# One encoder layer in float32 halves: TensorE's order, the place of the quarters' sums, the loads of the way out and the buffers of the mixer's squares

## The chip, the core and the metric

The kernel runs on one core of a Trainium2 chip. The metric is the device time of one execution in microseconds (us), as the median of several runs. Before the change it is 913.55 us (three runs, 912.46 to 914.88).

## What is computed

The reference is one layer of a bidirectional encoder over 528 tokens (512 and 16 meta tokens) of width 1024, batch 1, in float32:

```
h = concat(meta, x)
h = h + 0.5 * swiglu(rms_norm(h, norm_ffn1), w_ffn1_in, w_ffn1_out)
u = rms_norm(h, norm_mix) @ w_in
xc = conv(u[:, :512]);  y_lru = (scan_fwd(xc) + scan_bwd(xc)) * gelu(u[:, 512:1024])
y_four = fft2(u[:, 1024:]).real @ fourier_w + fourier_b
h = h + concat(rms_norm(y_lru), rms_norm(y_four)) @ w_out
h = h + 0.5 * swiglu(rms_norm(h, norm_ffn2), w_ffn2_in, w_ffn2_out)
out = rms_norm(h, norm_final)[16:]
```

The two feed-forwards have width 2816, which is 22 blocks ("f") of 128 columns for the gate and 22 for the up side.

## The kernel before, in words

**Halves.** Every operand of a matmul is split into a high and a low float32r part, and a product is three matmuls (`mm3`, L351): high by high, high by low, low by high. The high part of a weight is a ScalarE copy, the low part a VectorE subtraction (`split_w`, L89, whose instructions have lines L90 and L91; for plain blocks L333 and L334).

**Fast products in the feed-forward.** Most f blocks use a scheme with seven products instead of eight: the gate and up weights are four quarters, and seven products P1 to P7 of sums of quarters by sums of token halves give the result (`pair`, L584). The first three f blocks of the first feed-forward and the first two of the second are plain ("classic"). In the second feed-forward the way out of four chunks of four f blocks uses the same scheme (`way_out`, L649), and the first chunk (two f blocks) and the last one use plain products.

**A block's weights.** `pair_loads` (L100) brings a pair of f blocks' columns in with five DMAs into three raw buffers a, b, c: up's first half into c, gate into b, up into a (SP's queue), and then two accumulating DMAs from POOL's queue, gate's first half onto c (L108) and gate's second half onto b's first (L109). `pair_blocks` (L112) splits a, and the second half of b into the tiles jh and jl. It gives the weights of P1, P2 and P4. `pair_sums` (L122) adds c's first half to b's second half (L126), splits b, and forms c's second half from a and b (L129). It gives P6 and P5. `pair_differences` (L132) splits c for P7 and P3.

**Jobs.** All weights are a list of jobs, in the order in which they are used (`ffn_jobs`, L263). `block()` (L339) hands out the next one, keeps loads six jobs ahead (`FETCH`) and splits three jobs ahead (`LOOK`). There are seven raw buffers of 1024 columns (`wraw`) and five pairs of split tiles (`wsp`). Every plain job takes one raw buffer and one pair, however few columns it has. The way out of the first chunk of the second feed-forward is eight jobs (one for each of eight output blocks d) of 2 x 128 columns. The last chunk (`tail`, L1170) takes four jobs of 1024 columns, two outputs in each.

**The order of work.** The kernel is written with a tile framework. It takes the instructions in the order in which the program traces them, plans for each engine an order from expected times, lets an instruction whose inputs are expected move ahead of one whose inputs are not, and sets the semaphores. `tc.keep_in_program_order` ties an instruction behind the one traced before it on the same engine. In the second feed-forward the first matmul of each product group is tied so (`onto`, L569, which passes `pinned` to `mm3`):

```
            mm = nc.tensor.matmul(o, wh, xh[i], start=first, stop=False, skip_group_check=go_on)
            if pinned:
                tc.keep_in_program_order(mm)
...
                    mm3([ps], w[0][:, k], w[1][:, k], [xh], [xl], first and k == 0, k == nk - 1, True, not lead and k == 0)
```

In the first feed-forward (`lead` is set) and everywhere else TensorE's matmuls are not tied. The written order of the second feed-forward's steps is `schedule2` (L227): P1, P2, P6, P7, P5, P4, P3 of a block with way-out products of the chunk before between them. P4 adds onto the bank C that P7 wrote and that VectorE reads at L611, after P5 and ScalarE's copy L610. P3 adds onto the bank A that L610 reads.

**The mixer's norms.** `add_square` (L450) squares a block on ScalarE (L458) into a temporary and adds it to a running sum on VectorE (L459). For the LRU half (L1099) the temporary is the tag "sq" with one buffer. For the Fourier half (L1076) it is in turn that one and the tag "t" of the mixer's pool (two buffers, also used for convolutions, folds and the spread root). After the sums, TensorE adds over partitions (L467), ScalarE and VectorE take the reciprocal root, and TensorE spreads it (L485).

Of the kernel before, what the change touches and what calls it, by code (L numbers as in the profile page):

```python
# [9 lines left out]
F32 = mybir.dt.float32  # L10
# [4 lines left out]
P = 128  # L15
# [50 lines left out]
def encoder_layer(ctx: ExitStack, tc: tile.TileContext, xT, vecs, w1i, w1o, wm, wg, wo, w2i, w2o, w2q,  # L66
# [45 lines left out]
    def pair_blocks(pair):  # L112

        a, b, _ = pair["raw"]
        hi, lo = w_tiles()
        split_w(hi, lo, a)
        jh = state["pool"].tile([P, 512], F32R, tag="jh", name="jh")
        jl = state["pool"].tile([P, 512], F32R, tag="jl", name="jl")
        split_w(jh, jl, b[:, 512:])
        return [(quarter(hi, 0), quarter(lo, 0)), (quarter(hi, 1), quarter(lo, 1)), (quarter(jh, 0), quarter(jl, 0))]  # L120

    def pair_sums(pair):  # L122

        a, b, c = pair["raw"]

        tc.keep_in_program_order(nc.vector.tensor_tensor(b[:, 512:], b[:, 512:], c[:, :512], op=ALU.add))  # L126
        hi, lo = w_tiles()
        split_w(hi, lo, b)
        nc.vector.tensor_tensor(c[:, 512:], a[:, 512:], b[:, 512:], op=ALU.add)  # L129
        return [(quarter(hi, 0), quarter(lo, 0)), (quarter(hi, 1), quarter(lo, 1))]  # L130
# [132 lines left out]
    def ffn_jobs(wi, wo_, wq, steps):  # L263
        pairs = {}
        for step in steps:
            kind, f, d = step[:3]
            if kind == "out" and (len(step) == 3 or step[3] == 0):
                jobs.append((wo_[d][:, f[0]:f[1], :], P, f[1] - f[0], P, 8))
            elif kind == "tail":
                for dp in range(ND // 2):  # L270
                    src = wo_[2 * dp:2 * dp + 2, :, f[0]:f[1], :].rearrange("d p f m -> p d (f m)")
                    jobs.append((src, P, 2, (f[1] - f[0]) * P, 8))
            elif kind == "classic":
                for b in range(2):
                    jobs.append((wi[f, b], P, 8, P, 2 if len(jobs) < 3 else 8))
            elif kind == "in" and d in ("P1", "P6", "P7"):
                pair = pairs.setdefault(f, {"src": (wi[f, 1], wi[f, 0])})
                jobs.append(({"P1": pair_blocks, "P6": pair_sums, "P7": pair_differences}[d], pair))
            elif kind == "so" and d in ("P1", "P6"):
                quad = pairs.setdefault(("so", f), {"src": wq[f[0], f[2]] if d == "P1" else None})  # L280
                jobs.append((quad_blocks if d == "P1" else quad_sums, quad))
# [68 lines left out]

    def mm3(outs, wh, wl, xh, xl, first, last, go_on=False, pinned=False):  # L351

        for i, o in enumerate(outs):
            mm = nc.tensor.matmul(o, wh, xh[i], start=first, stop=False, skip_group_check=go_on)  # L354
            if pinned:
                tc.keep_in_program_order(mm)
        for i, o in enumerate(outs):
# [92 lines left out]
    def add_square(ss, src, n, first, tag="sq"):  # L450
        if first:
            nc.scalar.activation(ss[:, :n], src, AF.Square)
        else:
            if isinstance(tag, str):
                sq = tmp.tile([P, T], F32, tag=tag, bufs=1, name="sq")
            else:
                sq = tag.tile([P, T + 4], F32, tag="t", bufs=2, name="sq")
            nc.scalar.activation(sq[:, :n], src, AF.Square)  # L458
# [11 lines left out]
    def rstd_of(q, name, pool=None):  # L470
        r = tmp.tile([P, T], F32, tag="rstd", bufs=1, name=name) if pool is None else pool.tile([P, T + 4], F32, tag="t", bufs=2, name=name)
        m, k = q.shape
# [27 lines left out]
    def ffn(X, R, t0, n, steps, on_done, tail, lead, sums, hook):  # L500
        half = n // 2
        with tc.tile_pool(name="ffn", bufs=10 if lead else 3) as fp, tc.tile_pool(name="ffnt", bufs=2) as ft:
# [66 lines left out]
            def onto(ps, w, x, first):  # L569

                nk = w[0].shape[1]
                for k in range(nk):
                    xh, xl = x(k)
                    mm3([ps], w[0][:, k], w[1][:, k], [xh], [xl], first and k == 0, k == nk - 1, True, not lead and k == 0)

# [156 lines left out]
            first = []  # L732
            out = {}
            for step in steps:
# [24 lines left out]
                else:  # L759
                    if len(step) == 3 or step[3] == 0:  # L760
                        out[d] = banks(n, "po"), block()
                    ps, (wh, wl) = out[d]
                    for k, j in enumerate(range(*f)):
                        if len(step) == 3 or step[3] == k:
                            ah, al = acts[j]
                            ah, al = flat(ah), flat(al)
                            mm3(ps, wh[:, k], wl[:, k], halves(ah, n), halves(al, n), k == 0, j == f[1] - 1)
                            last = j == f[1] - 1
                    if not last:
                        continue  # L770
                    for hl, p in zip(halves(h[d][:, t0:], n), ps):
# [83 lines left out]
    with tc.tile_pool(name="mx", bufs=1) as mx, tc.tile_pool(name="mt", bufs=2) as mt:  # L855
# [219 lines left out]
        for c in range(NL):  # L1075
            add_square(ssf, yf[c][:, META:T], SEQ, c == 0, mt if c % 2 else "sq")  # L1076

# [19 lines left out]
        for c, gt in enumerate(gates):  # L1097
            nc.vector.tensor_tensor(hs[c], hs[c], gt, op=ALU.mult)
            add_square(ssl, hs[c], SEQ, c == 0)  # L1099

# [69 lines left out]
    def tail(acts, temps):  # L1170
        blocks = []
        for _ in range(ND // 2):
            parts = [x.rearrange("p d (f m) -> p d f m", m=P) for x in block()]
            blocks += [[x[:, e] for x in parts] for e in range(2)]
        nt = len(acts)
# [180 lines left out]
```

## Time and profile before

| what | value |
|---|---|
| median of three runs | 913.55 us |
| profiled execution | 917.13 us, its span 915.3 us |
| TensorE clock granted, mean | 0.991 |
| ScalarE busy | 478.9 us, 52% of the span |
| GpSimd busy | 96.7 us, 11% |
| DMA | 125.20 MB in 53744 packets, 137 GB/s |

A profile is of one execution. TensorE is PE (its weight loads PEld), VectorE DVE, ScalarE ACT, GpSimd POOL, SyncE SP; L126 is line 126 of the kernel. The clock is the share of TensorE's full speed that was granted in a stretch. Matmuls are pipelined and their ends are modelled, so counts of matmuls in a stretch tell more than the busy time does.

### The profile page before, as it was taken

To read this page: it belongs to the slowest core of one execution; us is meant where nothing else is said; L and a number is where in the kernel's file an instruction comes from. 1 tells how busy PE (TensorE), PEld (TensorE's weight loads), DVE (VectorE), ACT (ScalarE), POOL (GpSimd) and SP (SyncE) were. 2 spreads that over 40 slices of the span, in tenths; PEclk is the share of its full clock that TensorE was granted. 3 is DMA by queue.
4 is the path that set the end of the run, shared out by engine and by line. 5 is a ranking of instruction groups with operands and counts; after the bars stand their busy time and mean duration, and the time that the engine had idled before them with its cause. 6 is when DMAs were issued, how large, how long until landed. Compare 5 with 4: busy or idle time off the path is not lost.

```text
span 915.3 us, 17225 instructions
## 1 busy us (share of the span) xinstructions
PE 873.1 (95%) x6854; PEld 848.2 (93%) x6854; DVE 705.1 (77%) x1227; ACT 478.9 (52%) x766; POOL 96.7 (11%) x114
## 2 busy tenths in 40 slices
PE   8999999999999999999898999899898998898996
PEld 8999999999999999999777899798898998898996
DVE  7988765867767767678985688688878969968854
ACT  7665433534444435588545354465545545555544
POOL 0111010010010000000000000111212121131100
PEclk9999999999999999999998999999999999999998
DMA  8747653564664433431423311675586785685512
GB/s 299 180 119 189 167 150 81 159 165 105 173 161 123 132 100 114 139 106 59 138 93 81 77 33 30 184 193 154 136 217 138 161 198 139 168 203 134 159 22 92
DMA packets 53744, 125.20 MB, mean 137 GB/s; under 512 B 5920, under 2 KB 12832, under 8 KB 53664
## 3 DMA queue, kind: packets, MB, share of 16 engines
q1 hardware_dynamic: 37280, 96.84, 33.6%
q0 software_dynamic: 15840, 26.75, 18.1%
q8 instruction: 53, 0.87, 0.4%
q10 hardware_dynamic: 544, 0.52, 0.2%
q14 instruction: 27, 0.22, 0.1%
HBM read 115.70 MB, written 2.10 MB: 129 GB/s over the span
## 4 chain that ended last, share of the span: by engine, by line
PE 71%; DVE 18%; ACT 4%; issue 4%; DMA 2%; SPq 1%; DVEq 0%; ACTq 0%
PE pp L354 14%; PE pp L360 13%; PE pp L358 13%; PE po L354 5%; PE po L360 5%; PE po L358 5%; DVE wlo L91 4%; PE pw L358 2%; PE pm L354 2%; PE pm L360 1%; PE pm L358 1%; PE pw L360 1%; PE pw L354 1%; ACT whi L90 1%; DVE al L411 1%
## 5 line engine op out<-in xcount | busy, mean ns | idle before, releaser
L90 ACT ACTIVATE whi<-raw 128x1024 fp32r<-128x1024 f32 (+1 forms) x149 | 150.6, 1032 | 73.5 <-DVE raw L126 35.6
L91 DVE TENSOR_TENSOR wlo<-raw,whi 128x1024 fp32r<-128x1024 f32 (+1 forms) x149 | 175.4, 1192 | 17.2 <-ACT whi L90 17.1
L360 PE MATMUL pp<-th,wlo 128*128 128x256 f32 (+1 forms) x468 | 132.7, 284 | 3.2 <-DVE wlo L91 3.2
L354 PE MATMUL pp<-th,whi 128*128 128x256 f32 (+1 forms) x468 | 133.4, 285 | 1.2 <-ACT whi L90 0.6
L358 PE MATMUL pp<-xl,whi 128*128 128x256 f32 (+1 forms) x468 | 132.5, 283 | 0.0
L360 PE MATMUL pp<-xh,wlo 128*128 128x256 f32 (+1 forms) x468 | 132.5, 283 | 0.0
L354 PE MATMUL pp<-xh,whi 128*128 128x256 f32 (+1 forms) x468 | 132.3, 283 | 0.0
L358 PE MATMUL pp<-tl,whi 128*128 128x256 f32 (+1 forms) x468 | 132.1, 282 | 0.0
L333 ACT ACTIVATE whi<-raw 128x512 fp32r<-128x512 f32 (+3 forms) x95 | 69.4, 740 | 60.0 <-PE po L358 23.4
L360 PEld LDWEIGHTS pp<-th,wlo 128*128 128x128 f32 x468 | 88.0, 188 | 3.9 <-DVE wlo L91 3.9
L354 PEld LDWEIGHTS pp<-th,whi 128*128 128x128 f32 x468 | 88.2, 189 | 2.7 <-ACT whi L90 1.0
L334 DVE TENSOR_TENSOR wlo<-raw,whi 128x512 fp32r<-128x512 f32 (+3 forms) x95 | 78.2, 827 | 13.6 <-ACT whi L333 12.4
L354 PEld LDWEIGHTS pp<-xh,whi 128*128 128x128 f32 x468 | 88.3, 189 | 0.0
L360 PEld LDWEIGHTS pp<-xh,wlo 128*128 128x128 f32 x468 | 88.2, 189 | 0.0
L358 PEld LDWEIGHTS pp<-tl,whi 128*128 128x128 f32 x468 | 88.2, 188 | 0.0
L358 PEld LDWEIGHTS pp<-xl,whi 128*128 128x128 f32 x468 | 88.1, 188 | 0.0
L354 PE MATMUL po<-ah,whi 128*128 128x264 f32 (+1 forms) x368 | 78.8, 292 | 3.1 <-ACT whi L333 3.0
L360 PE MATMUL po<-ah,wlo 128*128 128x264 f32 (+1 forms) x368 | 78.2, 290 | 0.9 <-DVE wlo L334 0.9
L358 PE MATMUL po<-al,whi 128*128 128x264 f32 (+1 forms) x368 | 78.6, 291 | 0.0
L360 PE MATMUL pp<-ah,wlo 128*128 128x256 f32 x224 | 63.7, 285 | 3.9 <-DVE wlo L91 3.9
L354 PE MATMUL pp<-ah,whi 128*128 128x256 f32 x224 | 64.1, 286 | 1.2 <-ACT whi L90 0.7
L358 PE MATMUL pp<-al,whi 128*128 128x256 f32 x224 | 63.2, 282 | 0.0
(254 smaller groups left out, 2180.2 us busy)
## 6 DMA issues: line engine op xcount, KB each, us to landing
raw<-in_w2i SPq DMA_DIRECT2D x44, 512.0 KB, 4.4
raw<-in_w1i SPq DMA_DIRECT2D x41, 512.0 KB, 4.3
raw<-in_w2i POOLq DMA_DIRECT2D x40, 256.0 KB, 3.9
raw<-in_w1i POOLq DMA_DIRECT2D x38, 256.0 KB, 4.9
raw<-in_w1o SPq DMA_DIRECT2D x32, 256.0 KB, 3.1
raw<-in_w2q SPq DMA_DIRECT2D x16, 512.0 KB, 5.3
raw<-in_wm SPq DMA_DIRECT2D x12, 512.0 KB, 3.6
raw<-in_w2i SPq DMA_DIRECT2D x20, 256.0 KB, 3.4
```

The costliest lines, as they stand in the source:

```text
L90: nc.scalar.activation(hi, raw, AF.Copy)
L91: nc.vector.tensor_tensor(lo, raw, hi.bitcast(F32), op=ALU.subtract)
L333: nc.scalar.activation(hi[:p, s], raw[:p, s], AF.Copy)
L334: nc.vector.tensor_tensor(lo[:p, s], raw[:p, s], hi[:p, s].bitcast(F32), op=ALU.subtract)
L354: mm = nc.tensor.matmul(o, wh, xh[i], start=first, stop=False, skip_group_check=go_on)
L358: nc.tensor.matmul(o, wh, xl[i], start=False, stop=False, skip_group_check=go_on)
L360: nc.tensor.matmul(o, wl, xh[i], start=False, stop=last, skip_group_check=go_on)
L411: nc.vector.tensor_tensor(lo, src, hi.bitcast(F32), op=ALU.subtract)
```

## The change

It does four things. It takes the `pinned` parameter out, so that no matmul is tied in the second feed-forward. It moves the two additions of `pair_sums` into `pair_blocks`, behind the split of jh and jl; the first one stays tied to VectorE's traced order. It makes the way out of the second feed-forward's first chunk two jobs of 1024 columns, four outputs in each, which a new `blocks_of` hands out one by one (the tail uses it too). And it gives the mixer's squares two buffers "sq" of their own in the mixer's pool, and the spread roots two "root" buffers; both no longer use "t", and the LRU half's squares no longer the single "sq". The rest is the removal of a case that no step uses.

```diff
     def pair_blocks(pair):
 
-        a, b, _ = pair["raw"]
+        a, b, c = pair["raw"]
...
         split_w(jh, jl, b[:, 512:])
+
+        tc.keep_in_program_order(nc.vector.tensor_tensor(b[:, 512:], b[:, 512:], c[:, :512], op=ALU.add))
+        nc.vector.tensor_tensor(c[:, 512:], a[:, 512:], b[:, 512:], op=ALU.add)
...
     def pair_sums(pair):
 
-        a, b, c = pair["raw"]
-
-        tc.keep_in_program_order(nc.vector.tensor_tensor(b[:, 512:], b[:, 512:], c[:, :512], op=ALU.add))
         hi, lo = w_tiles()
-        split_w(hi, lo, b)
-        nc.vector.tensor_tensor(c[:, 512:], a[:, 512:], b[:, 512:], op=ALU.add)
+        split_w(hi, lo, pair["raw"][1])
...
-            if kind == "out" and (len(step) == 3 or step[3] == 0):
+            if kind == "out" and not wq:
                 jobs.append((wo_[d][:, f[0]:f[1], :], P, f[1] - f[0], P, 8))
-            elif kind == "tail":
-                for dp in range(ND // 2):
-                    src = wo_[2 * dp:2 * dp + 2, :, f[0]:f[1], :].rearrange("d p f m -> p d (f m)")
-                    jobs.append((src, P, 2, (f[1] - f[0]) * P, 8))
+            elif kind == "tail" or kind == "out" and d == 0:
+                m = (f[1] - f[0]) * P
+                n = 1024 // m
+                for dp in range(0, ND, n):
+                    jobs.append((wo_[dp:dp + n, :, f[0]:f[1], :].rearrange("d p f m -> p d (f m)"), P, n, m, 8))
...
-    def mm3(outs, wh, wl, xh, xl, first, last, go_on=False, pinned=False):
+    several = []
+
+    def blocks_of():
+
+        if not several:
+            parts = [x.rearrange("p d (f m) -> p d f m", m=P) for x in block()]
+            several.extend([x[:, e] for x in parts] for e in range(parts[0].shape[1]))
+        return several.pop(0)
+
+    def mm3(outs, wh, wl, xh, xl, first, last, go_on=False):
 
         for i, o in enumerate(outs):
-            mm = nc.tensor.matmul(o, wh, xh[i], start=first, stop=False, skip_group_check=go_on)
-            if pinned:
-                tc.keep_in_program_order(mm)
+            nc.tensor.matmul(o, wh, xh[i], start=first, stop=False, skip_group_check=go_on)
...
-                sq = tag.tile([P, T + 4], F32, tag="t", bufs=2, name="sq")
+                sq = tag.tile([P, T], F32, tag="sq", bufs=2, name="sq")
...
-        r = tmp.tile([P, T], F32, tag="rstd", bufs=1, name=name) if pool is None else pool.tile([P, T + 4], F32, tag="t", bufs=2, name=name)
+        r = tmp.tile([P, T], F32, tag="rstd", bufs=1, name=name) if pool is None else pool.tile([P, T], F32, tag="root", bufs=2, name=name)
...
-                    mm3([ps], w[0][:, k], w[1][:, k], [xh], [xl], first and k == 0, k == nk - 1, True, not lead and k == 0)
+                    mm3([ps], w[0][:, k], w[1][:, k], [xh], [xl], first and k == 0, k == nk - 1, True)
...
-                    if len(step) == 3 or step[3] == 0:
-                        out[d] = banks(n, "po"), block()
-                    ps, (wh, wl) = out[d]
+                    ps, (wh, wl) = banks(n, "po"), block() if lead else blocks_of()
...
-            add_square(ssf, yf[c][:, META:T], SEQ, c == 0, mt if c % 2 else "sq")
+            add_square(ssf, yf[c][:, META:T], SEQ, c == 0, mt)
...
-            add_square(ssl, hs[c], SEQ, c == 0)
+            add_square(ssl, hs[c], SEQ, c == 0, mt)
...
     def tail(acts, temps):
-        blocks = []
-        for _ in range(ND // 2):
-            parts = [x.rearrange("p d (f m) -> p d f m", m=P) for x in block()]
-            blocks += [[x[:, e] for x in parts] for e in range(2)]
+        blocks = [blocks_of() for _ in range(ND)]
```

## Rows read from the trace of the kernel before

**Rows 1.** The page, part 1: busy us and share of the span of each engine.

```profile
PE 873.1 (95%) x6854; PEld 848.2 (93%) x6854; DVE 705.1 (77%) x1227; ACT 478.9 (52%) x766; POOL 96.7 (11%) x114
```

**Rows 2.** Stretches: length, busy us (instructions) of each engine, clock, DMA share, GB/s.

```profile
61.00:345.00 284.00, 283.84 (x2321) 283.10 (x2320) 206.99 (x340) 125.77 (x190) 26.91 (x31) 1.00 0.55 143
479.00:490.70 11.70, 11.57 (x50) 8.86 (x48) 10.51 (x16) 9.19 (x14) 0.00 (x0) 1.00 0.23 69
490.70:495.50 4.80, 2.03 (x10) 1.66 (x8) 1.82 (x2) 2.86 (x3) 0.87 (x1) 0.75 0.40 82
495.50:500.40 4.90, 4.90 (x13) 3.90 (x14) 0.18 (x1) 0.26 (x1) 0.86 (x1) 0.55 0.39 117
540.00:564.70 24.70, 23.74 (x200) 23.77 (x201) 22.69 (x49) 13.33 (x23) 0.00 (x0) 1.00 0.06 17
564.70:581.80 17.10, 13.24 (x50) 9.84 (x49) 10.95 (x20) 6.10 (x11) 0.00 (x0) 0.90 0.20 57
581.80:616.00 34.20, 33.07 (x276) 32.62 (x275) 27.24 (x43) 17.28 (x28) 6.96 (x8) 1.00 0.84 223
616.00:662.00 46.00, 41.84 (x343) 40.81 (x343) 40.43 (x70) 26.05 (x41) 7.90 (x9) 1.00 0.59 147
662.00:682.00 20.00, 20.00 (x169) 19.93 (x168) 16.28 (x30) 11.22 (x18) 4.39 (x5) 1.00 0.92 222
```

**Rows 3.** Timeline of ScalarE, 486 to 493 us: start, us, what, idle before and releaser.

```profile
487.81 0.63 ACT L458 ACTIVATE sq<-t 128x512 f32<-128x512 f32 x1 [0.22 <-DVE ss L459]
490.88 1.06 ACT L333 ACTIVATE whi<-raw 128x1024 fp32r<-128x1024 f32 x1 [2.44 <-PE pw L358]
491.84 0.61 ACT L458 ACTIVATE sq<-t 128x512 f32<-128x512 f32 x1
```

**Rows 4.** Timeline of TensorE, 486 to 505 us, a wait.

```profile
493.85 1.87 PE L467 MATMUL sums<-consts,ss 128*128 128x1 f32 x8 [2.77 <-DVE ss L459]
```

**Rows 5.** Timeline of SyncE's queue, 500 to 640 us: the loads of the way out.

```profile
539.07 36.55 SPq L306 DMA_DIRECT2D raw<-in_w2o  x8
```

**Rows 6.** Timeline of ScalarE, 568 to 581 us.

```profile
574.39 0.42 ACT L333 ACTIVATE whi<-raw 128x256 fp32r<-128x256 f32 x1 [4.49 <-DMA raw<-in_w2o]
```

**Rows 7.** DMA issues: count, KB each, median us to landing.

```profile
raw<-in_w2i SPq DMA_DIRECT2D x44, 512.0 KB, 4.4
...
raw<-in_w2o SPq DMA_DIRECT2D x8, 128.0 KB, 2.0
```

**Rows 8.** Waits of TensorE, 581 to 862 us: us in total, times, longest.

```profile
PE pp L354 <- DVE q L611: 9.9, 10, 1.6
PE pp L360 <- DVE wlo L91: 7.1, 7, 1.3
```

**Rows 9.** Timeline of TensorE, 632 to 662 us, three of its waits.

```profile
636.50 0.39 PE L360 MATMUL pp<-ah,wlo 128*128 128x256 f32 x1 [0.96 <-DVE wlo L91]
...
641.34 0.39 PE L354 MATMUL pp<-th,jh 128*128 128x256 f32 x1 [1.27 <-DVE q L611]
...
653.52 0.39 PE L360 MATMUL pp<-th,wlo 128*128 128x256 f32 x1 [0.95 <-DVE wlo L91]
```

**Rows 10.** Timeline of VectorE, 24 to 34 and 620 to 664 us.

```profile
26.53 0.68 DVE L91 TENSOR_TENSOR jl<-raw,jh 128x512 fp32r<-128x512 f32 x1
...
633.62 0.69 DVE L91 TENSOR_TENSOR jl<-raw,jh 128x512 fp32r<-128x512 f32 x1
...
635.23 2.08 DVE L91 TENSOR_TENSOR wlo<-raw,whi 128x1024 fp32r<-128x1024 f32 x2
...
650.17 0.69 DVE L126 TENSOR_TENSOR raw<-raw 128x512 f32<-128x512 f32 x1
```

**Rows 11.** Timeline of GpSimd, 18 to 34 and 540 to 640 us: accumulating transfers issued.

```profile
21.91 1.02 POOL L108 DMA_DIRECT2D raw<-in_w1i  x1 [21.46 <-DMA raw<-in_w1i]
...
621.00 0.86 POOL L108 DMA_DIRECT2D raw<-in_w2i  x1 [12.29 <-DMA raw<-in_w2i]
```

**Rows 12.** Line L108, the first accumulating transfer of each block: time to landing.

```profile
DMA to landing us min/median/max: 3.5/3.9/7.7
```

More of the change, by code (lines that the diff above doesn't have):

```diff
@@ L732, in ffn @@
             first = []
-            out = {}
             for step in steps:
@@ L759, in ffn @@
                 else:
-                    if len(step) == 3 or step[3] == 0:
-                        out[d] = banks(n, "po"), block()
-                    ps, (wh, wl) = out[d]
+                    ps, (wh, wl) = banks(n, "po"), block() if lead else blocks_of()
                     for k, j in enumerate(range(*f)):
[L764 to L770, printed above, removed]
+                        ah, al = [flat(x) for x in acts[j]]
+                        mm3(ps, wh[:, k], wl[:, k], halves(ah, n), halves(al, n), k == 0, j == f[1] - 1)
                     for hl, p in zip(halves(h[d][:, t0:], n), ps):
```

## The prediction

> **What bounds the kernel now.** I read the page first. TensorE is busy 95% of the span, the engine next to it, VectorE, 77% [rows 1], so the question is where TensorE runs below its pace. The stretches answer that [rows 2]. From 61 to 345 us, the first feed-forward block, it has no idle time: 2321 matmuls in 284 us, 0.122 us each. Nothing is pinned there. In the second block a light stretch (662 to 682) runs 169 matmuls in 20 us, 0.118 us each, and that is the pace I measure the rest by. Three places fall short.
>
> First, the mixer's norm. In 4.8 us from 490.7 only 10 instructions run, and in the 4.9 us after it 13 run at a granted clock of 0.55 [rows 2]. TensorE waits 2.77 us for the last add into ss [rows 4]. On ScalarE the second square through the one "sq" buffer waits for VectorE's add, and the third stands behind a weight split that waits 2.44 us for TensorE [rows 3].
>
> Second, the way out of the first two f blocks: 564.7 to 581.8 holds its 48 products of 512 columns (8 outputs x 2 f blocks x 3) in 17.1 us, with a clock of 0.90 [rows 2]. Its eight loads are spread over 36.55 us [rows 5], and ScalarE waits 4.49 us for one of them [rows 6], though one lands in 2.0 us [rows 7]. The buffers are the cause: two blocks that are fetched ahead hold six of the seven raw buffers, so each 256-column load waits until the load before it has been split.
>
> Third, the rest of the second block. From 581 to 862 us the two largest waits of TensorE are for the add of L611 and for low halves (L91) [rows 8]. One period shows them in place [rows 9]: at 636.5 a low half, at 641.3 the add, at 653.5 a low half. From 616 to 662 us there are 343 matmuls in 46 us; at 0.118 they need 40.6, so 5.4 are lost [rows 2]. The pattern comes four times (616, 682, 747 and 813 us). From 581.8 to 616 us, 276 matmuls need 32.7 of 34.2: 1.5 lost. Together 4 x 5.4 + 1.5 = 23.1 us. VectorE is nearly full in that heavy stretch: 40.43 us of 46, and 16.28 of 20 in the light one [rows 2].
>
> **The change part by part.**
>
> *Own buffers for squares.* With two "sq" buffers the second square needs no add, and the third needs the add that held the second one before, at 487.81 [rows 3]. That is 3 us ahead of the split at 490.88, if ScalarE's planned order lets it go first. Then the last add ends near 490, and the sums need not wait: 2.8 us [rows 4]. The half-clock stretch behind the wait goes too: 12 products of 512 columns take 4.9 us there, and at the pace ahead of 490.7 (50 in 11.70 us, 0.234 each [rows 2]) 2.8: 2.1 us. Sum 4.9. Bounds: 0, where the split keeps its place before the third square, and 4.9. I take 4.9, since nothing else in those rows holds the squares. The final reciprocal root and its spread hide behind the next products as they do now. Moving the other squares off the "t" buffers I cost at nothing: TensorE has projections to run there.
>
> *Way out by 1024 columns.* Eight loads, eight ScalarE and eight VectorE splits of 256 columns become two of 1024. A 512 KB load lands in 4.4 us [rows 7]; the first is issued at 539, the second when the first is split, near 557, so it lands near 562 and feeds the fifth of eight outputs, near 570. The wait and the half clock go: 48 x 0.234 = 11.2 us against 17.1, 5.9 us. SP issues six DMAs fewer, and the raw buffers come free earlier for the next blocks. Against this, VectorE has 2.8 us more to do before 565 (next part), where it is busy 22.69 of 24.7 us [rows 2] and has 2.0 left: 0.8 late. Sum 5.1; bounds 2 (a second load that comes as late as the worst ones now, for half the outputs) and 5.9.
>
> *Sums with the first three blocks.* Nothing is added: two VectorE adds of 0.69 us move from the preparation of P6 to that of P1. In the row's period they go from 650.17 and the next to it to just behind the low half at 633.62 [rows 10]. P6's split then no longer waits for them, and the raw buffer of "up" is free some 17 us earlier, so SP's and POOL's queues move up too. The price: the low half at 635.23, for which TensorE waits at 636.5 [rows 9], would start 1.4 us later, four times: 5.6 us. The gain is the wait at 653.5, 0.95 us, four times: 3.8. Lasting bounds are thus -5.6 and +3.8; I take 0, because a free order of products (next part) can cover the later split. For the first two blocks of the second feed-forward the adds (2.8 us) land between 541 and 545 us, which is the 0.8 above.
> The accumulating transfer that the add reads was issued at 621.00 [rows 11] and at the longest landing of 7.7 us [rows 12] is there by 628.7, five us before the add would run; by these rows the move makes no wait. Only at the very start can it: the transfer issued at 21.91 [rows 11] may land as late as 29.6, and the low half before the add begins at 26.53 [rows 10], so VectorE may stand up to 2.4 us. TensorE has 144 classic products of the first blocks to run then (17.6 us at 0.122), which hide it; without them it would cost 2.4, and I take 0. The Trainium skill's page "Perfetto Trace Analysis", section "Per-engine timelines", says that VectorE takes its instructions strictly first in, first out, which speaks against the move: an add whose transfer is late holds every split behind it. By that rule alone the sum would lose wherever a transfer is late; no row shows one so late.
>
> *Order no longer pinned.* The pin ties the first product of each group (P1 to P7 of a block and of a way-out square) behind all products before it. Without it the framework, when it plans the order, may put any product ahead whose inputs it expects. While P4 waits for L611, P3 needs only ScalarE's copy, and the next way-out products need only their weights; while a low half is late, P5 or the next block's P1 can run. So there is work for each of the waits. But VectorE must supply it: without the 5.4 us the heavy stretch would be 40.6 us long with 40.43 of VectorE work in it, 99.6%. Over heavy and light stretch together it would be 56.7 of 60.6, 94%, so part of the work has to move over, as far as five split buffers and seven raw ones allow. Bounds: 0 (the waits are VectorE's and stay) and 23.1 (all go). I take 60%, 13.9 us: nearer to the upper end, because in the unpinned first block no TensorE time is lost, and short of it for VectorE's sake. Should a stall go, the low halves are late next.
>
> Sum: 4.9 + 5.1 + 13.9 = 23.9 us. The profiled execution took 917.13 us, 3.6 more than the median of the runs, 913.55. 917.1 - 23.9 = 893.2; on the median's scale 889.6.
>
> **The rivals.**
>
> *All waits go.* For it: the unpinned first block. Against it: VectorE at 94%. It gains 23.1 + 10.0 = 33.1: 880.5 on the median's scale, within 877 to 884.
>
> *VectorE is the bound.* The order changes but the products still wait for low halves, which come as before. For it: 40.43 of 46 us, and two waits of three are for VectorE's splits or adds. It leaves 0 to 7 us of the third part's 23.1: 913.6 - 10.0 - 4 = 899.6 in the middle, 897 to 906 with the low bounds of the first two parts.
>
> *A product planned ahead of its turn stops the queue (slower).* The order is fixed at build time by expected times. If the planner puts a product early and its weights come later on the chip, everything behind it stands, and no pin keeps it behind. Place: the five chunks of the second block. Price: as at 490.7, a wait of 2.8 us and 2.1 lost at half clock, 4.9 us. One in each chunk, and nothing gained in the third part, gives 24.5 - 10 = 14.5: 928; two in each give 953. It decides once three such stalls stand without a gain in the third part: then they eat the 10 us of the first two. For it: TensorE stands at 490.7 and in the way out with unpinned products, so its planned order is not always right. Against it: the first block. The Trainium skill's page "TensorE: Matmul & The Clock Gate", section "Step-by-step: what each phase is for", says that the queue pulls only weight loads ahead and that matmuls stay in program order; the trace agrees, since no product ran during the 2.77 us of that wait [rows 4].
>
> *It changes nothing.* The planner finds the same order, and ScalarE's order keeps the split ahead of the square; new small waits eat what the loads bring: 911 to 916.
>
> **How the numbers follow.** Forecast (7 to 19 us of the third part, 884 to 897) 0.48; all waits go 0.15; VectorE the bound 0.22; nothing 0.04; slower 0.11. A measurement of this kernel can tell about 0.3%, 2.7 us, from no change. Faster by more: 0.48 + 0.15 + 0.22 = 0.85; within it 0.04; slower 0.11. The range 876 to 906 takes in the first three cases, 0.85, with the bounds of the single terms.
>
> **What the profile after would show.** Squares right: no wait of TensorE for ss before the second half's sums, and the clock at 1.00 there. Loads right: two loads of w2o of 512 KB ahead of the tail's, and 48 products of 512 columns in 11 to 12 us. Sums right: L126's successor directly behind the low half of each third quarter, and ScalarE no longer waiting for it. Order right: P4 no longer directly behind P5 and two way-out products, waits for L611 under a third of the 9.9 us now, and VectorE busy over 90% of the four periods. The forecast is wrong if TensorE's waits in the second block stay above 15 us, or if new waits on DMA or on ScalarE's high halves appear there.

## The result, and the profile after

The changed kernel takes 889.71 us, the median of four runs (889.41 to 891.26), against 914.21 of the kernel before beside it: ratio 0.9738, 95% interval 0.9718 to 0.9757. Its profiled execution is the one of 889.71 us, span 887.9. The profiled execution of before (917.13) was 2.9 us above its median, this one is on its own, so 27.4 us less in the two spans stand for 24.5 in the medians.

Lines have moved: L121 and L122 are the sums (L126, L129 before), L363/L365/L367 the three matmuls of `mm3`, L376 a product (`times`), L417/L418 the split of an activation (L410, L411), L465/L466 square and add, L474 the sums over partitions, L618 the add of P4 (L611). L90/L91 and L333/L334 are still the weight splits.

The page, part 1, which answers to [rows 1]:

```profile
PE 869.8 (98%) x6854; PEld 847.1 (95%) x6854; DVE 700.1 (79%) x1221; ACT 476.4 (54%) x760; POOL 96.7 (11%) x114
```

Stretches of the changed kernel, against [rows 2] (columns: stretch, length; busy us and instructions of PE, PEld, DVE, ACT, POOL; granted clock, DMA share, GB/s):

```profile
61.00:345.00 284.00, 283.79 (x2321) 283.01 (x2321) 207.78 (x341) 125.96 (x191) 25.90 (x30) 1.00 0.55 140
490.70:495.50 4.80, 4.80 (x31) 4.17 (x30) 1.41 (x2) 2.60 (x3) 0.87 (x1) 1.00 0.45 102
534.00:558.80 24.80, 23.59 (x199) 23.62 (x200) 24.31 (x49) 13.25 (x20) 1.73 (x2) 1.00 0.38 96
561.70:574.50 12.80, 12.78 (x48) 10.05 (x49) 9.45 (x14) 2.32 (x4) 1.75 (x2) 0.87 0.61 151
574.60:605.00 30.40, 30.32 (x255) 30.11 (x254) 21.27 (x34) 15.35 (x24) 3.47 (x4) 1.00 0.52 130
605.00:645.00 40.00, 39.96 (x333) 39.40 (x332) 36.32 (x65) 24.14 (x38) 6.13 (x7) 1.00 0.62 161
666.00:727.00 61.00, 60.92 (x506) 60.11 (x505) 53.69 (x96) 35.28 (x57) 14.10 (x16) 1.00 0.78 185
```

The first block is the same to 0.05 us of TensorE. From 574.6 to the tail at 850 the view lists no wait of TensorE: 40 us hold 333 matmuls, 0.120 each, where before 46 us held 343. VectorE, the feared bound, is at 36.32 of 40 there and at 53.69 of 61 (88%) over a full period.

TensorE's waits after 470 us, all that the view lists (engine and line, releaser: us in total, times, longest); the two of [rows 8] are gone, and a new one leads; the last is at the very end, in the final norm:

```profile
PE po L363 <- ACT ah L417: 2.6, 1, 2.6
PE sums L474 <- DVE ss L466: 1.5, 1, 1.5
PE pss L492 <- DVE root L1225: 0.6, 1, 0.6
```

**The norm.** Timeline of ScalarE, 484 to 495 us (start, us, what, idle before and releaser), against [rows 3]:

```profile
486.07 1.24 ACT L465 ACTIVATE sq<-t 128x512 f32<-128x512 f32 x2
487.22 1.05 ACT L333 ACTIVATE whi<-raw 128x1024 fp32r<-128x1024 f32 x1
488.17 0.61 ACT L465 ACTIVATE sq<-t 128x512 f32<-128x512 f32 x1
490.98 1.06 ACT L333 ACTIVATE whi<-raw 128x1024 fp32r<-128x1024 f32 x1 [2.20 <-PE pw L365]
```

The third square now stands ahead of the split that waits for TensorE. VectorE's last add into ss starts at 489.70 and takes 0.68, and the sums run at 491.01 without a wait.

**The way out.** Its two loads are issued one behind the other (SyncE's queue, start, us between first and last):

```profile
533.32 5.79 SPq L306 DMA_DIRECT2D raw<-in_w2o  x2
```

They are early, against 36.55 us [rows 5], and no weight is late. But the first product waits for an activation and the clock falls behind it. Timeline of TensorE:

```profile
561.72 1.41 PE L363 MATMUL po<-ah,whi 128*128 128x512 f32 x4 [2.63 <-ACT ah L417]
...
563.85 0.63 PE L363 MATMUL po<-ah,whi 128*128 128x512 f32 x1
...
565.96 0.40 PE L363 MATMUL po<-ah,whi 128*128 128x512 f32 x1
```

Steps of 0.42 us from 563.4 to 566.0, 0.23 behind it: the half clock (1.2 of 2.4 GHz). What ScalarE and VectorE did before it, and, last, TensorE's first product of P1 of the fast blocks, from which the text below counts:

```profile
553.92 1.04 ACT L90 ACTIVATE whi<-raw 128x1024 fp32r<-128x1024 f32 x1
...
556.76 1.05 ACT L90 ACTIVATE whi<-raw 128x1024 fp32r<-128x1024 f32 x1
...
559.12 1.08 ACT L714 ACTIVATE q<-pg 128x512 f32<-128x512 f32 x2
560.09 1.06 ACT L90 ACTIVATE whi<-raw 128x1024 fp32r<-128x1024 f32 x1
561.04 1.15 ACT L417 ACTIVATE ah<-q 128x512 fp32r<-128x512 f32 x2
...
558.45 1.22 DVE L91 TENSOR_TENSOR wlo<-raw,whi 128x1024 fp32r<-128x1024 f32 x1
559.75 1.29 DVE L376 TENSOR_TENSOR q<-pu,q 128x512 f32<-128x512 f32 x2
560.96 1.21 DVE L91 TENSOR_TENSOR wlo<-raw,whi 128x1024 fp32r<-128x1024 f32 x1
562.09 1.29 DVE L418 TENSOR_TENSOR al<-q,ah 128x512 fp32r<-128x512 f32 x2
...
553.23 0.28 PE L363 MATMUL pp<-xh,whi 128*128 128x256 f32 x1
```

On ScalarE three weight splits stand ahead of ah: P6's of the first two fast blocks (553.92 and 556.76) and the next in the list of jobs, P7's of the first (560.09). On VectorE P6's low halves are at 558.45 and 560.96. Their products run only behind the 48 of the way out. What TensorE waits for is ah, so it is ScalarE's order that counts: ah starts 7.81 us after the first product of P1 (561.04 against 553.23). The Trainium skill's page "Perfetto Trace Analysis", section "Per-engine timelines", has ScalarE and VectorE take their instructions strictly first in, first out; the trace agrees, since q, whose last product into pg starts at 552.75, comes on ScalarE only at 559.12, behind two of the splits.

**Where the time came from.** Marks of the profiled executions in us, with the runs' medians and ratios (A: first product after the norm, `pw` from yl; B: first product of the way out; C: the product behind its 48th; D: first product of the tail, `pt`):

```
kernel                 median  ratio [95%]             A       B       C       D       B-A    C-B    D-C    span
before                 914.21                          504.08  564.71  581.84  877.40  60.63  17.13  295.56 915.3
after                  889.71  0.9738 [0.9718,0.9757]  498.38  561.72  574.60  850.25  63.34  12.88  275.65 887.9
b1_unpin               898.46  0.9808 [0.9789,0.9827]  503.86  564.40  580.74  859.10  60.54  16.34  278.36 896.9
b2_sums_early          908.20  0.9914 [0.9901,0.9927]  504.13  566.32  577.71  869.70  62.19  11.39  291.99 907.5
b3_loads_1024          908.47  0.9924 [0.9902,0.9947]  501.31  562.31  573.61  867.65  61.00  11.30  294.04 905.4
b4_squares             911.79  0.9947 [0.9929,0.9966]  498.52  560.63  577.71  871.93  62.11  17.08  294.22 909.7
a1_pins_back           907.65  0.9910 [0.9892,0.9928]  498.37  563.30  576.11  868.09  64.93  12.81  291.98 905.8
a2_sums_late           888.82  0.9706 [0.9687,0.9725]  498.29  559.32  570.58  848.95  61.03  11.26  278.37 887.2
a3_loads_256           887.40  0.9690 [0.9671,0.9709]  499.24  561.26  572.64  848.22  62.02  11.38  275.58 886.0
a4_squares_back        894.16  0.9767 [0.9748,0.9786]  503.32  566.66  579.47  855.00  63.34  12.81  275.53 892.6
r_after                889.76  0.9714 [0.9695,0.9733]  498.44  561.79  574.38  849.96  63.35  12.59  275.58 887.6
c1_two_late            887.42  0.9687 [0.9668,0.9705]  498.41  560.89  572.18  847.75  62.48  11.29  275.57 885.6
c3_p6_tied             887.35  0.9685 [0.9672,0.9698]  498.13  560.59  571.83  847.75  62.46  11.24  275.92 885.5
c2_two_late_norm       885.50  0.9667 [0.9654,0.9679]  498.23  558.85  570.11  845.74  60.62  11.26  275.63 884.1
```

Against before the change gains 5.70 us up to A, loses 2.71 between A and B, gains 4.25 from B to C and 19.91 from C to D, and 0.26 behind D: 27.4.

### The profile page after: what moved, and what is told of

It reads as the page before. It is cut to its first block, busy times and chain, and to the rows that moved or that the text cites. A ratio compares the mean times of both kernels' runs of the same rounds, so it can differ in the third digit from the quotient of the medians.

```text
span 887.9 us, 17188 instructions
## 1 busy us (share of the span) xinstructions
PE 869.8 (98%) x6854; PEld 847.1 (95%) x6854; DVE 700.1 (79%) x1221; ACT 476.4 (54%) x760; POOL 96.7 (11%) x114
## 4 chain that ended last, share of the span: by engine, by line
PE 83%; DVE 10%; ACT 4%; issue 2%; DMA 1%; SPq 1%; DVEq 0%; ACTq 0%
PE pp L363 17%; PE pp L365 16%; PE pp L367 16%; PE po L363 5%; PE po L365 5%; PE po L367 5%; PE pm L365 2%; PE pm L363 2%; PE pm L367 2%; PE pw L365 2%; PE pw L367 1%; PE pw L363 1%; DVE wlo L91 1%; ACT whi L90 1%; PE pt L363 1%
## 5 line engine op out<-in xcount | busy, mean ns | idle before, releaser
L90 ACT ACTIVATE whi<-raw 128x1024 fp32r<-128x1024 f32 (+1 forms) x149 | 150.9, 1032 | 85.1 <-PE po L365 32.7
L91 DVE TENSOR_TENSOR wlo<-raw,whi 128x1024 fp32r<-128x1024 f32 (+1 forms) x149 | 176.3, 1193 | 10.8 <-ACT whi L90 9.8
L363 PE MATMUL pp<-xh,whi 128*128 128x256 f32 (+1 forms) x468 | 132.5, 285 | 1.3 <-ACT whi L90 0.5
L363 PE MATMUL pp<-th,whi 128*128 128x256 f32 (+1 forms) x468 | 133.3, 285 | 0.3
L365 PE MATMUL pp<-xl,whi 128*128 128x256 f32 (+1 forms) x468 | 132.5, 283 | 0.0
L367 PE MATMUL pp<-xh,wlo 128*128 128x256 f32 (+1 forms) x468 | 132.3, 283 | 0.0
L365 PE MATMUL pp<-tl,whi 128*128 128x256 f32 (+1 forms) x468 | 132.0, 282 | 0.0
L367 PE MATMUL pp<-th,wlo 128*128 128x256 f32 (+1 forms) x468 | 131.9, 283 | 0.0
L333 ACT ACTIVATE whi<-raw 128x512 fp32r<-128x512 f32 (+3 forms) x89 | 68.2, 777 | 51.9 <-PE po L365 23.8
L363 PEld LDWEIGHTS pp<-xh,whi 128*128 128x128 f32 x468 | 88.0, 189 | 3.2 <-ACT whi L90 1.5
L363 PEld LDWEIGHTS pp<-th,whi 128*128 128x128 f32 x468 | 88.2, 188 | 1.6 <-ACT q L599 1.2
L365 PEld LDWEIGHTS pp<-tl,whi 128*128 128x128 f32 x468 | 88.2, 188 | 0.0
L367 PEld LDWEIGHTS pp<-xh,wlo 128*128 128x128 f32 x468 | 88.2, 188 | 0.0
L365 PEld LDWEIGHTS pp<-xl,whi 128*128 128x128 f32 x468 | 88.1, 188 | 0.0
L367 PEld LDWEIGHTS pp<-th,wlo 128*128 128x128 f32 x468 | 87.9, 188 | 0.0
L334 DVE TENSOR_TENSOR wlo<-raw,whi 128x512 fp32r<-128x512 f32 (+3 forms) x89 | 77.2, 873 | 11.7 <-ACT whi L333 10.7
L363 PE MATMUL po<-ah,whi 128*128 128x264 f32 (+1 forms) x368 | 78.1, 291 | 2.7 <-ACT ah L417 2.6
L365 PE MATMUL po<-al,whi 128*128 128x264 f32 (+1 forms) x368 | 78.6, 291 | 0.0
L367 PE MATMUL po<-ah,wlo 128*128 128x264 f32 (+1 forms) x368 | 78.3, 291 | 0.0
L363 PE MATMUL pp<-ah,whi 128*128 128x256 f32 x224 | 63.7, 288 | 0.0
L365 PE MATMUL pp<-al,whi 128*128 128x256 f32 x224 | 63.0, 282 | 0.0
L367 PE MATMUL pp<-ah,wlo 128*128 128x256 f32 x224 | 62.3, 283 | 0.0
```

The source lines that it names most:

```text
L90: nc.scalar.activation(hi, raw, AF.Copy)
L91: nc.vector.tensor_tensor(lo, raw, hi.bitcast(F32), op=ALU.subtract)
L333: nc.scalar.activation(hi[:p, s], raw[:p, s], AF.Copy)
L334: nc.vector.tensor_tensor(lo[:p, s], raw[:p, s], hi[:p, s].bitcast(F32), op=ALU.subtract)
L365: nc.tensor.matmul(o, wh, xl[i], start=False, stop=False, skip_group_check=go_on)
L367: nc.tensor.matmul(o, wl, xh[i], start=False, stop=last, skip_group_check=go_on)
```

## The experiments

The runs came in three groups, each beside runs of the kernel before (medians 915.37, 916.67 and 915.66). "a" and "c" kernels are the changed kernel edited, "b" kernels the one before. A gain of a "b" kernel is given by its ratio; the medians alone differ by 18.2 us (b1), 7.5 (b2), 8.2 (b3) and 3.9 (b4).

**The free order: a1_pins_back and b1_unpin.** The same lines, put back into the one and taken out of the other:

```diff
-            nc.tensor.matmul(o, wh, xh[i], start=first, stop=False, skip_group_check=go_on)
+            mm = nc.tensor.matmul(o, wh, xh[i], start=first, stop=False, skip_group_check=go_on)
+            if pinned:
+                tc.keep_in_program_order(mm)
```

> The changed kernel with the first matmul of each product group tied again in the second feed-forward, all else as changed. Theory 1 (the free order of TensorE brings the 20 us gained between the first P6 and the tail): the four periods go back from 61.1 to about 65 us, the kernel to 905 to 911. Theory 2 (the early sums bring them, since P6's split no longer waits for L126 and a raw buffer is free sooner): the periods stay under 62.5 us, the kernel under 896. Both needed: in between, and the run with late sums shows as much.

> The kernel before with the ties taken away and nothing else. Theory 1 (the free order alone removes the waits of the four periods): the waits after 582 us go, 17 to 21 us less than before on the same chip (894 to 898), with the waits at 493 and 574 us still there. Rival (it takes the early sums too): 5 to 12 us less.

Measured: with the pins back, 907.65 us, 17.9 more than the changed kernel; with nothing but the pins gone, 0.9808, that is 17.6 of 916.67 less. C to D takes 291.98 us against 275.65, and 278.36 against 295.56: 16.3 and 17.2. (b1_unpin's 898.46 is 0.5 above the 894 to 898 expected, the difference within its 17 to 21; its waits at 493 and near 574 us stay, 2.8 and 2.6.) TensorE's waits from 577 us to the tail (total, times, longest), a1_pins_back:

```profile
PE pp L363 <- DVE q L620: 8.3, 9, 1.6
PE pp L369 <- DVE wlo L91: 4.9, 4, 1.2
PE pp L363 <- DVE hall L669: 1.7, 3, 0.6
```

and b1_unpin, where the second still belongs to the way out:

```profile
PE pp L354 <- ACT sq L685: 1.4, 3, 0.5
PE po L358 <- DVE wlo L334: 0.9, 1, 0.9
```

The waits for the add of P4 and for the low halves of L91 are there in each kernel with the pins and in none without. The free order alone is the larger part of the gain.

**The sums: a2_sums_late and b2_sums_early.** The two adds back into `pair_sums` of the changed kernel, or moved into `pair_blocks` of the one before:

```diff
     def pair_blocks(pair):
...
+        tc.keep_in_program_order(nc.vector.tensor_tensor(b[:, 512:], b[:, 512:], c[:, :512], op=ALU.add))
+        nc.vector.tensor_tensor(c[:, 512:], a[:, 512:], b[:, 512:], op=ALU.add)
```

> The changed kernel with both sums back in the preparation of P6. Theory 1: the periods stay near 61 us; ahead of the way out VectorE has 2.8 us less to do, so TensorE's wait of 3.0 us for the activations at 561.7 shrinks to under 1 us, and the kernel takes 885 to 889. Theory 2: the periods go back to 64 us or more and the kernel to 900 or more.

> Kernel before with the quarters' sums early and nothing else. Theory (early sums free the buffer of the up side, so the way out's eight 256-column loads no longer stand behind one another; the pins stay, so the waits of the second feed-forward stay): the way out's 48 products take 11 to 13 us instead of 16.9 to 17.1, the stretch from the first P6 to the tail's first product stays within 3 us of the kernel before's 295.6, total 4 to 7 us less, 908 to 912. Rival (the early sums cost as much in the pinned stretch as they save, because low halves come 1.4 us later with no other product to run): within 2.7 us of the kernel before, or slower.

Measured: the changed kernel with late sums takes 888.82, 0.9 less: its wait for ah is 0.3, it reaches C 4.0 us earlier (570.58 against 574.60) and takes 2.7 more from C to D. The kernel before with early sums is 7.9 us faster (0.9914): B to C takes 11.39 instead of 17.13, and C to D 291.99 instead of 295.56. The second is 0.6 us more than its theory allowed, and the total gain is over its 4 to 7; the rival, by which the pinned stretch would lose what the sums save, falls. In b2_sums_early the two largest waits from C to the tail, and one of the second kind (the place of 636.50 in [rows 9]), are

```profile
PE pp L353 <- DVE q L610: 8.4, 9, 1.6
PE pp L359 <- DVE wlo L91: 4.9, 4, 1.2
...
631.73 0.39 PE L359 MATMUL pp<-ah,wlo 128*128 128x256 f32 x1 [1.23 <-DVE wlo L91]
```

against 9.9 (10 times) and 7.1 (7 times) in [rows 8]: three of the waits for low halves, those behind the late add, go (0.95, 0.96 and 1.33 us before). The four that stay have grown from 0.96 to 0.99 us each to 1.23, 1.0 us in sum, and three new ones of 0.6 for an add of the way out (L659) come, 1.7 in sum: a part of the rival's price, less than what the sums save. Its eight 256-column loads are still spread over 30.29 us, but no split of ScalarE in the way out waits for one until 571.43 (1.24 us), and TensorE does not.

**The loads: a3_loads_256 and b3_loads_1024.** The way out's eight loads put back, or the two large ones alone:

```diff
-            if kind == "out" and not wq:
+            if kind == "out":
...
-            elif kind == "tail" or kind == "out" and d == 0:
+            elif kind == "tail":
```

> The changed kernel with the way out of the first chunk as eight jobs of 256 columns again. If the eight serial loads were the cause of the waits at 574 and 579 us before: those waits are back (a wait for the high half of 2 to 4 us, half clock after it), and the kernel takes 893 to 897. Rival (the free order runs P6 in such a wait, so that the loads no longer matter): within 1.5 us of 889.7.

> The kernel before with the way out of the first chunk as two jobs of 1024 columns and nothing else. Theory 1 (the serial small loads make the waits at 574 and 579 us): 48 products of 512 columns in 11 to 12.5 us instead of 17, 908 to 911 us. Rival (two fetched blocks hold six raw buffers in any case, so the second large load is late too): 912 or more.

Measured: alone on the kernel before the large loads give 7.0 us (0.9924), B to C 11.30 instead of 17.13. Taken out of the changed kernel they give 2.3 more: 887.40, with 11.38 from B to C and no wait for ah. Neither expectation had that: by the first the changed kernel loses by it, by the rival it stays within 1.5 us. In a3_loads_256 no split of 1024 columns stands between 550.6 and ah (560.57) on ScalarE, only way-out splits of 256 columns (0.42 us each); in b3_loads_1024, with late sums, TensorE waits 0.26 for ah. Large loads and early sums are two cures of one stall, with early sums the large loads have nothing left to cure, and the new wait needs both.

**The squares: a4_squares_back and b4_squares.** The old temporaries put back, or the new ones alone:

```diff
-                sq = tag.tile([P, T], F32, tag="sq", bufs=2, name="sq")
+                sq = tag.tile([P, T + 4], F32, tag="t", bufs=2, name="sq")
...
-            add_square(ssl, hs[c], SEQ, c == 0, mt)
+            add_square(ssl, hs[c], SEQ, c == 0)
```

> The changed kernel with the mixer's squares in the buffers of before. If the one buffer made the wait of 2.8 us and the half clock after it: both are back at 493 us and the kernel takes 894 to 896. Rival (the gain of 5.7 us there comes from another planned order, not from the buffers): within 1.5 us of 889.7.

> Kernel before with the mixer's squares on buffers of their own and nothing else (the new way of handing out the way out's blocks is in it, its loads stay at 256 columns). Theory (the wait of 2.77 us for the last add and the half clock behind it go, and the rest stays): no wait of over 1 us between 488 and 500 us, the first product after the norm 4.5 to 5.7 us earlier, total 4 to 6 us less, 909 to 912. Rival (the gain exists only with the free order, since the pinned products behind it wait anyway): within 1.5 us of the kernel before.

Measured: 4.5 us (894.16 against 889.71) and 4.9 (0.9947 of 915.66; 3.9 by the medians). A comes 4.9 and 5.6 us earlier, and in a4_squares_back the wait of 2.77 is back. In b4_squares 1.5 of this is lost again between A and B to a half clock at 534 to 540 us (below). The rival, that the pinned products behind it wait anyway, falls.

**The new wait: r_after, c1_two_late and c3_p6_tied.** r_after is the changed kernel once more, beside c1_two_late, in which the first two fast blocks of the second feed-forward form their sums late:

```diff
+        if not pair["late"]:
+            quarter_sums(a, b, c)
...
     def pair_sums(pair):
+        if pair["late"]:
+            quarter_sums(*pair["raw"])
...
-                pair = pairs.setdefault(f, {"src": (wi[f, 1], wi[f, 0])})
+                pair = pairs.setdefault(f, {"src": (wi[f, 1], wi[f, 0]), "late": wq is not None and f < CHUNKS2[0] + 2})
```

> The changed kernel itself once more, beside the others of this set: 889 to 891 us by every theory. It shows whether 887.4 us with eight loads is a difference of the kernels or of the measurements.

> The changed kernel with the two sums late (in the preparation of P6) for the first two fast blocks of the second feed-forward alone; all others early. Theory 1 (the 2.8 us of sums ahead of the way out make TensorE's wait of 3.0 us for the activations and the half clock after it, while the early sums bring 2.7 us later on, from the first P6 to the tail): the wait is under 0.8 us, first P6 near 570.6, and 275 to 276 us from there to the tail's first product; 883.5 to 886.5 us. Rival (the wait comes from splits of P6's weights that are planned ahead of the activations): the wait stays over 2 us and the kernel over 888.

Measured: r_after repeats the marks within 0.3 us. c1_two_late takes 887.42; the wait for ah is 0.2, B to C 11.29, and C to D keeps the early sums' 275.57. The total is 0.9 above what theory 1 allowed and below the rival's 888: its profiled run loses 1.5 us to a half clock at 534 to 540 (last section). The run leaves open whether the 2.8 us of adds or the place of P6's splits, which c1_two_late also moves, made the activations late. c3_p6_tied keeps the early sums and ties those splits alone:

```diff
-        split_w(hi, lo, pair["raw"][1])
+        if pair["late"]:
+            tc.keep_in_program_order(nc.scalar.activation(hi, pair["raw"][1], AF.Copy))
+            tc.keep_in_program_order(nc.vector.tensor_tensor(lo, pair["raw"][1], hi.bitcast(F32), op=ALU.subtract))
+        else:
+            split_w(hi, lo, pair["raw"][1])
```

> Changed kernel with P6's weight split of the first two fast blocks of the second feed-forward tied to its traced place on ScalarE and VectorE, so that it can't be planned ahead of the activations of the last plain block. Theory A (the new 3.0 us wait of TensorE for the high half of the activation at 561.7 us comes from these splits placed ahead of it): the wait is under 1 us, the 48 products of the way out take 11 to 12 us, total 886 to 888. Theory B (it comes from the 2.8 us of early sums that VectorE takes at 537 to 540 us): the wait stays at 1.5 to 3 us, total 888.5 to 891.

Measured: 887.35; ScalarE, VectorE and TensorE (the way out's first product, then P1's) in c3_p6_tied:

```profile
560.71 0.63 ACT L421 ACTIVATE ah<-q 128x512 fp32r<-128x512 f32 x1 [0.18 <-DVE q L380]
...
561.65 1.05 ACT L129 ACTIVATE whi<-raw 128x1024 fp32r<-128x1024 f32 x1
...
559.18 1.50 DVE L380 TENSOR_TENSOR q<-pu,q 128x512 f32<-128x512 f32 x2
560.60 1.47 DVE L422 TENSOR_TENSOR al<-q,ah 128x512 fp32r<-128x512 f32 x2
...
562.74 1.23 DVE L130 TENSOR_TENSOR wlo<-raw,whi 128x1024 fp32r<-128x1024 f32 x1 [0.33 <-ACT whi L129]
...
560.59 1.19 PE L367 MATMUL po<-ah,whi 128*128 128x512 f32 x4 [0.18 <-ACT ah L421]
...
554.54 0.28 PE L367 MATMUL pp<-xh,whi 128*128 128x256 f32 x1
```

The adds are where they were (L121 and L122, 536.53 to 539.03); the splits (L129, L130) now stand behind the activations, and the wait falls from 2.63 to 0.18. This profile has a half clock at 534 to 540 (below), which makes TensorE some 1.3 us late for the way out; that could shorten the wait too. a1_pins_back, with the same half clock (0.72) and the splits ahead, says that it does not (its wait is 2.63):

```profile
554.80 0.28 PE L363 MATMUL pp<-xh,whi 128*128 128x256 f32 x1
...
562.61 1.15 ACT L419 ACTIVATE ah<-q 128x512 fp32r<-128x512 f32 x2
```

From P1's first product to ah it is 7.81 us here and in the changed kernel, 5.36 in c3_p6_tied, and 5.46 in a2_sums_late (553.17 to 558.63). So the order of the splits costs 2.4 us, and the early adds on VectorE nothing that shows. Theory A holds: the planner had put splits whose buffers were ready ahead of activations that were due sooner.

**The norm's places: c2_two_late_norm.** c1_two_late, with two parts of the norm's second half, the sums and the spread, placed three and two steps later among the products of the second feed-forward's plain blocks (the expectation calls these places otherwise):

```diff
-NORM_1 = [(0, 7), (1, 2)]
+NORM_1 = [(1, 2), (1, 4)]
```

> Changed kernel with the sums late for the first two fast blocks of the second feed-forward (as in c1_two_late), and two of the places at which the mixer's way out runs norm steps moved one output later. Theory (in c1 the 1.5 us wait for the sum of squares near 535 us and the half clock behind it cost 1.5 us, and squares get more time with later places): no wait over 0.5 us there, clock 1.00 from 534 to 540 us, 884 to 886.5. Rival (the wait moves to the second place, or the half clock there comes from elsewhere): 887 to 889.

Measured: 885.50, 0.9667 [0.9654, 0.9679], 4.2 us below the changed kernel. The 534 to 540 us stretch of c2_two_late_norm

```profile
534.00:540.00 6.00, 6.00 (x54) 6.00 (x53) 4.62 (x12) 1.47 (x4) 0.00 (x0) 1.00 0.32 87
```

and of c3_p6_tied, which has the old places:

```profile
534.00:540.00 6.00, 5.04 (x30) 5.08 (x31) 5.55 (x12) 0.81 (x3) 0.00 (x0) 0.72 0.34 96
```

54 matmuls instead of 30, and no wait for the sum of squares. A wait of 1.66 us for ah is back, since TensorE is now ready for the way out before 558 us while the activation starts at 558.17; no split of P6 or P7 stands ahead of it here. It is the only wait of TensorE that the view lists from 480 to 862 us.

## Why the prediction was right, and where it was not

The time was 889.6 forecast and 889.71 measured, inside the range, and the side was right. That the two agree to 0.1 us is luck: on the profile's own scale the forecast was 893.2 for what took 889.7. The steps were off by 3.5 us in sum (23.9 forecast, 27.4 measured), which the correction to the median (3.6) covered, and within the sum one part was 3.6 too large and another 6.0 too small. By steps:

- **What bounds it:** right. The three places named are those where the time came from, and the first block did not move.
- **Squares, 4.9 us:** 5.7 to A, for the reason given: the third square stands ahead of the split. It is worth 4.5 taken out of the changed kernel and 3.9 to 4.9 alone. The half-clock part is not there in each profile (last section).
- **Loads, 5.1 us:** mis-sized for the whole change; B to C and the wait ahead of it give 4.25 less 2.71, 1.5 us. The step that failed is "2.0 left: 0.8 late". It priced the amount of VectorE's work, and that cost nothing that shows; the order on ScalarE had no price: the early sums make P6's splits ready, the planner puts them ahead of the activations, and TensorE stands 2.63 us and then runs some seven products at half clock (562.93 to 565.96). c3_p6_tied shows it. A new wait on ScalarE's high halves was one of the signs by which the forecast would be wrong, and it appeared, once; and the 48 products took 12.88 us, not 11 to 12. The 5.9 before it was right where it stands alone: 5.8 in b3_loads_1024, whose second load is issued at 554.47, near the 557 reckoned (539.11 in the changed kernel). That early sums cure the same stall was half written ("the raw buffer of up is free some 17 us earlier") and not counted.
- **Sums, 0:** the lasting effect is a gain, 2.7 us with the free order and 3.6 with the pins, near the upper bound of 3.8. That bound counts the wait at 653.5 four times, the trace has it three times (3.2 us). Of the price of 5.6 about 1.0 appeared with the pins (four low halves, 1.23 for 0.96 to 0.99), and none with the free order. The two blocks at the start cost 4.0, which is the loads' loss. Net, a2_sums_late says 0.9 lost, so 0 was nearly right, out of two larger terms.
- **Free order, 13.9:** mis-sized, 17.2 alone (b1_unpin) and 16.3 beside the others. Of the 23.1 counted as lost, 19.9 came back with the sums' part. The step that failed is the 60%, taken "for VectorE's sake". Products could move, as reckoned: in the heavy place of the first period P5's last product starts at 627.95 and P4 at 633.39, 5.4 us later, with way-out squares and P3 in between, where before P4 stood right behind P5 and two way-out products and waited (641.34 in [rows 9]). And VectorE's work moved too: 36.32 in 40 us, not the 99.6% that an unchanged stretch would have needed. The sign "over 90% of the four periods" did not come: it is 91%, 88%, 88% and 82%.
- **Rivals:** "all waits go" is near for the third part and not for the way out. "VectorE is the bound" falls with b1_unpin. The slower case, a product or a split planned ahead of its turn, happened on ScalarE and VectorE once, at 4.2 us (2.63 of wait and 1.6 more from B to C than in c3_p6_tied), far from the three stalls from which it decides.

## What to carry to other kernels

A pin that keeps one engine in the written order costs what its inputs' lateness costs, each time; where other products have their inputs, freeing the order can return most of it (here 16 to 17 of the 23 us counted), even with the feeding engine near 90% busy. Two edits that cure one stall are not worth their sum, and the second one can make a new stall: each is worth trying without the other (here early sums with small loads took 2.3 us less than both, large loads with late sums 0.9). Where an engine has room in a stretch, look at the order in which a planner will use it: work whose buffers come free early is put ahead of work that is due sooner.

## What was not expected of the hardware

The clock does not answer to the same wait in the same way each time. In the kernel before, after 2.77 us of waiting [rows 4], the clock was 0.55 for 4.9 us [rows 2]. b3_loads_1024 has the same 2.77 us wait, and behind it

```profile
493.84 1.05 PE L477 MATMUL sums<-consts,ss 128*128 128x1 f32 x8 [2.77 <-DVE ss L469]
```

```profile
495.50:500.40 4.90, 4.90 (x27) 4.09 (x26) 1.05 (x2) 0.86 (x2) 0.86 (x1) 1.00 0.35 119
```

27 matmuls at full clock instead of 13, and A comes 2.8 us earlier for that alone. b2_sums_early, with the same wait, has 12 at a clock of 0.50. The wait of 1.5 us for the sum of squares at 535 to 541 us in turn is followed, over the next 6 us, by 0.72 (38 matmuls) in a1_pins_back, a3_loads_256, c1_two_late, c3_p6_tied, b2_sums_early and b4_squares and by 1.00 (51) in the seven other rows of the table that have it, with 51 matmuls in the 6 us ahead of it in all of them; in c1_two_late, 1.5 us of it remain at the end of the stage (P1 of its blocks starts at 554.83, in r_after at 553.29). The one kernel with two profiles, the changed one and r_after, has 1.00 in both, so that one kernel gives both answers is not shown. The Trainium skill's page "TensorE: Matmul & The Clock Gate", part 1 on the clock gate, says that the monitor behind the gate runs free of the kernel's start, so that the moment of a change differs; that fits these traces, but none of them shows the monitor. Profiles of two kernels can thus differ by 1.5 to 2.8 us at each such wait without a reason in the edit, and b3_loads_1024's profiled span owes 2.8 us of its gain to it. Its other five runs took 0.9 to 6.5 us longer than the profiled one (907.14), with a mean clock of 0.987 to 0.995 against 0.997, so its median of 908.47 probably owes less.
